# Fewer out-state weights in the attention, power 0 by ScalarE, pointer scalars in norm and softmax, h1 scaled by ScalarE

## The chip, the cores and the metric

The kernel runs on one core of a Trainium2 chip. The metric is device microseconds of one execution. TensorE (PE) multiplies, VectorE (DVE), ScalarE (ACT) and GpSimd (POOL) do the elementwise work, SyncE (SP) issues most of the DMAs. Every engine works through its own instructions in order.

## The reference, cut to what matters

Two layers share a residual stream of 512 latent tokens and 256 context tokens of width 1024, all in float32. Layer 0 is windowed attention with a sink logit (16 heads, 128 wide), layer 1 a bidirectional S5 state space (128 groups of 16 channels, 64 complex states, two directions). Each layer ends in `layer_norm(alpha * x + gate * ((y * silu(z)) @ w_out))`. The softmax takes the sink into its sum:

```python
def softmax_with_sink(s, sink):
    sk = jnp.broadcast_to(sink[None, :, :, None, None], s.shape[:-1] + (1,))
    return jax.nn.softmax(jnp.concatenate([s, sk], -1), axis=-1)[..., :-1]
```

The S5 recurrence is `h[t] = abar * h[t-1] + bbar @ u[t]`, `y[t] = Re(cmat @ h[t])`, from the left and from the right.

## The kernel before, in words

Every float32 product is three matmuls of a high and a low part (`mm3`, lines 155 to 157); the parts are made by a copy on ScalarE and a subtraction on VectorE (lines 145 and 146, 580 and 581). The S5 layer is computed in chunks of 8 tokens. For that it needs *in-state weights* (`gen_w`, 64 of them) and *out-state weights* (`gen_o`, 32 of them, indices q = 0 to 31), which depend on parameters alone and are built while layer 0 runs, mostly on GpSimd, and stored to device memory.

An out-state weight q takes two loads on SyncE's queue, gcb (line 905) and gpp, the powers 0 to 8 of the states (line 907); three small products for gbb (lines 919 to 921); and for each of two directions d three instructions over 4 x 9 x 16 = 576 elements (lines 931 to 933) that multiply coefficients with the nine powers into a tile gO, with a scratch tile gX that has one buffer. In the powers' table power 0 stands at place 0 for d = 0 and at place 8 for d = 1; its first part is +1 on partitions 0 to 63 and -1 on 64 to 127, its second part is 0. Eight of the nine places, all but power 0, go to device memory (line 936). A later step, `lag` (lines 941 to 958), multiplies gbb with eight of the nine places of gO on TensorE (line 948), adds on VectorE and stores a tile gK (line 958); after every eighth weight, eight more DMAs move the collected gK (line 974). Weights 3, 7 and 11 run on VectorE, the others on GpSimd.

Layer 0 has 48 attention pieces (8 pairs of heads, 6 blocks of queries), between which the projections are interleaved. Pieces 1 to 21 carry in-state weights. From piece 22 (`NW`) on, `bg` opens a pool "go" (`open_o`, with four buffers of gO) and issues out-state weights up to `min(QA, (n - NW + 1) * QA // (47 - NW))` after piece n; each new weight is followed by the lag of the one before it. In `att_s` a piece computes scores, their negative maximum nm (for the context blocks by lines 453 and 454), the exponentials and their sums (line 461), adds the sink's exponential (lines 463 and 464), takes the reciprocal and scales.

The output projection follows (`outproj0`): half 0 of the columns for blocks 0, 1, 2 together, then 3, 4 and 5; half 1 for 5, 4, 0 together, then 1, 2 and 3. After each block's body it calls `side`, which in its first `NB` calls issues the remaining out-state weights, from a second pool "go2" with three buffers of gO; the pool is closed with the last. When both halves of a block are there, `norm` takes mean and variance, and the reciprocal root by three Newton steps on one column per partition (lines 293 and 294); line 631 normalizes, and `make_h1` transposes the block, applies scale and shift (four of eight pieces on VectorE, line 1018, four on ScalarE, line 1020) and splits it (lines 1023 and 1024) for the input projection of layer 1 (`uproj_ctx`, `uproj`). The tiles U of that projection come from a pool "uu" that is opened on the same side of memory after go2 is closed.

The whole program is put in order by a scheduler with a cost model: a priority is the place in the program, and `high_priority` with a negative offset (-80 for weights, -50 for lags) moves an instruction back. It fixes each engine's order before the run; tiles that share memory bring waits with them.

Of the kernel before, what the change touches and what calls it, by code (L numbers as in the profile page):

```python
# [111 lines left out]
F32 = mybir.dt.float32  # L112
# [21 lines left out]
class K:  # L134
# [141 lines left out]
    def norm(self, rs, pool):  # L276
        nc = self.nc
        st = pool.tile([128, 3, 6], F32, name="st")
        for i, (r, _) in enumerate(rs):
            nc.vector.bn_stats(st[:, i], r)  # L280
        mv = pool.tile([128, 2], F32, name="mv")
        nc.vector.bn_aggr(mv, st[:, :len(rs)])

        xe = pool.tile([128, 3], F32, name="xe")
        nc.vector.scalar_tensor_tensor(xe, mv[:, 1:2].to_broadcast([128, 3]), 1e-5, self.nscale, op0=ALU.add, op1=ALU.mult)
        ih = pool.tile([128, 2], I32, name="ih")
        nc.vector.tensor_scalar(ih[:, 0:1], xe[:, 2:3].bitcast(I32), 1, None, op0=ALU.logical_shift_right)
        nc.vector.tensor_scalar(ih[:, 1:2], ih[:, 0:1], -1, MAGIC_Y, op0=ALU.mult, op1=ALU.add)
        y = ih[:, 1:2].bitcast(F32)
        nt = pool.tile([128, 6], F32, name="nt")  # L290
        for i in range(3):
            t, yn = nt[:, 2 * i:2 * i + 1], nt[:, 2 * i + 1:2 * i + 2]
            nc.vector.scalar_tensor_tensor(t, y, xe[:, i:i + 1], y, op0=ALU.mult, op1=ALU.mult)
            nc.vector.scalar_tensor_tensor(yn, t, -3.0, y, op0=ALU.add, op1=ALU.mult)
            y = yn
        return mv[:, 0:1], y

# [33 lines left out]
def layer0(k, bg, early, late):  # L331
# [92 lines left out]
    def att_s(p, q, kk, qb):  # L424

        lat = qb < 4
        kb0, kb1 = (max(0, qb - 1), min(4, qb + 2)) if lat else (0, 0)
        win = list(range(kb0, kb1))

        cols = win + [4, 5]  # L430
        nw = 128 * len(win)
        n = nw + 256
        qs = slice(qb * 128, qb * 128 + 128)
        mc = k.sp.tile([128, 2], F32, name="mx", bufs=8)
        nm = k.sp.tile([128, 2], F32, name="nm", bufs=8)
        sm = k.sp.tile([128, 2], F32, name="sm", bufs=8)
        P = [k.sp.tile([128, 640], F32, name="P", bufs=2 * DEPTH + 2) for h in range(2)]

        def scores(h, S, cs, m, o):
            mm3(S, q[h][0][:, qs], q[h][1][:, qs], kk[0][:, cs], kk[1][:, cs], True, True)  # L440
            w = cs.stop - cs.start
            if lat:

                first = o == nw
                nc.vector.tensor_tensor_reduce(P[h][:, o:o + w], S, mask[:, m:m + w], -SCALE,  # L445
                                               k.nsink[:, 2 * p + h:2 * p + h + 1] if first else mc[:, h:h + 1],
                                               op0=ALU.add, op1=ALU.min, accum_out=(mc if first else nm)[:, h:h + 1])
        Sc = k.ps.tile([128, 2, 256], F32, name="S", tag="S", bufs=2)
        for h in range(2):
            scores(h, Sc[:, h], C, 384, nw)  # L450
        hs = slice(2 * p, 2 * p + 2)
        if not lat:
            nc.vector.tensor_reduce(mc, Sc, axis=AX.X, op=ALU.max)
            nc.vector.scalar_tensor_tensor(nm, mc, -SCALE, k.nsink[:, hs], op0=ALU.mult, op1=ALU.min)
        for h in range(2 if lat else 0):
            Sw = k.ps.tile([128, 512], F32, name="S", tag="S", bufs=2)[:, :nw]
            scores(h, Sw, slice(kb0 * 128, kb1 * 128), 128 if qb == 0 else 0, 0)
        es = k.sp.tile([128, 2], F32, name="es", bufs=8)
        for h in range(2):
            src = P[h][:, :n] if lat else Sc[:, h]  # L460
            nc.scalar.activation(P[h][:, :n], src, AF.Exp, bias=nm[:, h:h + 1], scale=-1.0 if lat else SCALE, accum_out=sm[:, h:h + 1])  # L461
        for h in range(2):
            nc.scalar.activation(es[:, h:h + 1], nm[:, h:h + 1], AF.Exp, bias=k.sink[:, 2 * p + h:2 * p + h + 1])
        nc.vector.tensor_add(es, es, sm)
        nc.vector.reciprocal(es, es)  # L465
        for h in range(2):
            nc.scalar.activation(P[h][:, :n], P[h][:, :n], AF.Copy, scale=es[:, h:h + 1])  # L467
        return P, cols
# [423 lines left out]
def open_o(k, pool, q0, q1, gob):  # L892

    k.gob, k.dq = gob, q0
    k.dd = pool.tile([128, 16 * (q1 - q0)], F32, name="dd")
    k.nc.sync.dma_start(k.dd, k.a["dd"][:, 16 * q0:16 * q1])


def gen_o(k, pool, q):

    nc, a = k.nc, k.a
    n = DO if q < DQ else DP
    eng = nc.vector if q % n == n - 1 else nc.gpsimd
    cb = pool.tile([128, 4, 2, 4, 16], F32, name="gcb", bufs=2)
    nc.sync.dma_start(cb.rearrange("p t d g n -> p (t d g n)"), a["cb"][q])
    pp = pool.tile([128, 2, 80], F32, name="gpp", bufs=2)
    nc.sync.dma_start(pp, k.ppsc[q])
    dd = k.dd
    O = []
    bb = pool.tile([128, 8, 2, 16], F32, name="gbb", bufs=2)  # L910
    t = pool.tile([128, 4, 9, 16], F32, name="gX", bufs=1).rearrange("p g k n -> p (g k n)")
    by, bx = (t[:, 128 * i:128 * i + 128].rearrange("p (d g n) -> p d g n", d=2, g=4) for i in range(2))

    def qb(o):
        return pp[:, :, o:o + 4][:, :, :, None].to_broadcast([128, 2, 4, 16])

    def dup(t):
        return t.rearrange("p d g n -> p (d g) n")[:, :, None].to_broadcast([128, 8, 2, 16])
    eng.tensor_tensor(by, cb[:, 2], qb(72), op=ALU.mult)
    eng.tensor_tensor(bx, cb[:, 3], qb(76), op=ALU.mult)  # L920
    eng.tensor_tensor(bb, dup(by), dup(bx), op=ALU.add)
    for d in range(2):
        o = pool.tile([128, 4, 9, 16], F32, name="gO", bufs=k.gob)
        x = pool.tile([128, 4, 9, 16], F32, name="gX", bufs=1)

        def cc(t):
            return cb[:, t, d][:, :, None].to_broadcast([128, 4, 9, 16])

        def pb(o_):
            return pp[:, d, o_:o_ + 36].rearrange("p (g k) -> p g k", g=4)[:, :, :, None].to_broadcast([128, 4, 9, 16])  # L930
        eng.tensor_tensor(o, cc(0), pb(0), op=ALU.mult)  # L931
        eng.tensor_tensor(x, cc(1), pb(36), op=ALU.mult)  # L932
        last = eng.tensor_tensor(o, o, x, op=ALU.add)  # L933
        O.append(o)
        x0 = 1 - d
        nc.sync.dma_start(k.osc[q, :, :, :, d].rearrange("p u r x -> p (u r) x"),
                          o[:, :, x0:x0 + 8].rearrange("p g t n -> p g (t n)"))

    def lag(after=None):
        ps = k.ps.tile([128, 512], F32, name="lag", tag=k.lagtag[0], bufs=k.lagtag[1])  # L940

        def lh(d, g):
            return bb[:, 4 * d + g].rearrange("p a n -> p (a n)")

        for d in (1, 0):
            for g in range(4):
                rs = slice(32 * g, 32 * g + 32)
                m = nc.tensor.matmul(ps[rs, 128 * (1 - d):128 * (1 - d) + 128], lh(d, g), O[d][:, g, d:d + 8], start=True, stop=True)  # L948
                if g == 0 and d == 1 and after is not None and k.gob > 3:

                    k.tc.add_manual_dep(ins_of(m), ins_of(after).name,
                                        mybir.DependencyInfo(mybir.DependencyClass.NoSync, mybir.DependencyReason.DATA), reason="lag")
        K_ = pool.tile([128, 240], F32, name="gK", bufs=1)
        nc.scalar.activation(K_[:, 0:112], ps[:, 0:112], AF.Copy)
        nc.scalar.activation(K_[:, 128:240], ps[:, 144:256], AF.Copy)
        nc.vector.tensor_add(K_[:, 112:128], ps[:, 112:128], dd[:, 16 * (q - k.dq):16 * (q - k.dq) + 16])
        nc.vector.tensor_add(K_[:, 112:128], ps[:, 128:144], K_[:, 112:128])
        nc.sync.dma_start(k.ksc[q], K_)
        if q % 8 == 7:
            gen_m0(k, q // 8)  # L960
    return lag, last
# [42 lines left out]
def make_h1(k, b, n):  # L1004
# [4 lines left out]
    for j in range(2):  # L1009
# [4 lines left out]
        for i in range(4):  # L1014
            kk = 4 * j + i
            g, c = k.h1g[:, r, kk:kk + 1], k.h1b[:, r, kk:kk + 1]
            if j == 0:
                nc.vector.tensor_scalar(hf[:, kk], t[:, i], g, c, op0=ALU.mult, op1=ALU.add)
            else:
                nc.scalar.activation(hf[:, kk], t[:, i], AF.Identity, bias=c, scale=g)  # L1020
    H, Lo = k.H1[r]
    ts = slice((b - 4 * r) * 128, (b - 4 * r) * 128 + 128)
    nc.scalar.activation(H[:, :, ts], hf, AF.Copy)
# [308 lines left out]

N0, NW, EW = 1, 22, 8
QO, QN = 32, 1
QA, NB = 27, 3
PP = 300
GP = 80
XP = 100
# [251 lines left out]
```

## Time and profile before

| | |
|---|---|
| median of 3 runs | 1510.47 us (1504.64 to 1512.83) |
| the profiled execution's own time | 1508.56 us |
| its span | 1506.8 us |
| TensorE busy | 1404.2 us, 93% |
| VectorE busy | 1040.2 us, 69% |
| ScalarE busy | 645.8 us, 43% |
| GpSimd busy | 635.0 us, 42% |
| mean granted TensorE clock | 0.971 |

The span is from the first to the last instruction of the profiled execution. In the rows, PE, DVE, ACT, POOL and SPq are TensorE, VectorE, ScalarE, GpSimd and SyncE's queue; L933 is line 933 of the kernel; `gO<-gcb,gpp` means that gO is written and gcb and gpp are read. "Idle before, <- releaser" is the time that an engine stood still before an instruction, and what ended it. The clock is a share of full speed. The attention runs to about 670 us, the output projection to about 870 us, and layer 1 takes the rest; from 870 us on GpSimd has next to nothing to do until the last projection.

### The profile page before, as it was taken

Reading aid. Unit: us, or ns where it says so; the run is one execution under the profiler, and the core shown is the slowest. Engines: PE = TensorE matmul, PEld = TensorE weight load, DVE = VectorE, ACT = ScalarE, POOL = GpSimd, SP = SyncE. Lnnn points to the kernel's source line nnn. Section 1 sums busy time; section 2 is a strip of 40 time slices with the busy share of each in tenths; the row PEclk is TensorE's granted clock in tenths of the full one; section 3 lists DMA queues with packets and bytes.
Section 4 is the critical chain, followed back from the end, with each engine's and each line's share of the span. In section 5 each row is a group of like instructions: output and inputs, shape, how many; then the busy total and the mean of one; then the engine's idle time right before and its main releaser. Section 6 shows DMA issues by size and latency. Waiting matters only on the chain.

```text
span 1506.8 us, 25662 instructions
## 1 busy us (share of the span) xinstructions
PE 1404.2 (93%) x9092; PEld 1134.5 (75%) x9092; DVE 1040.2 (69%) x2711; ACT 645.8 (43%) x1256; POOL 635.0 (42%) x542
## 2 busy tenths in 40 slices
PE   7999999999997899987988799999999999999997
PEld 2554789988886788875766688888777777888886
DVE  7734748777684477876759922789887896565376
ACT  1310546555464446552333234445556545343220
POOL 0004469999998676988975800000000000000240
PEclk9999999999998899998999899999999999999999
DMA  9876566766664446488795476667666796655541
GB/s 335 274 232 203 163 192 202 225 214 208 200 221 152 131 146 200 141 248 265 214 280 158 137 257 226 210 210 231 220 226 220 223 292 213 197 195 168 180 152 60
DMA packets 252639, 309.57 MB, mean 205 GB/s; under 512 B 45408, under 2 KB 151648, under 8 KB 252512
## 3 DMA queue, kind: packets, MB, share of 16 engines
q1 hardware_dynamic: 227168, 295.36, 61.5%
q10 hardware_dynamic: 25344, 12.59, 2.9%
q8 instruction: 71, 1.16, 0.3%
q14 instruction: 56, 0.46, 0.1%
HBM read 239.20 MB, written 77.07 MB: 210 GB/s over the span
## 4 chain that ended last, share of the span: by engine, by line
PE 54%; POOL 13%; DVE 13%; DMA 10%; issue 5%; ACT 3%; SPq 1%; POOLq 0%; DVEq 0%; ACTq 0%
PE pg L155 4%; PE pg L157 4%; PE pg L156 4%; PE adaps L166 3%; PE po L156 3%; PE po L157 3%; PE po L155 3%; DMA wsc<-gW 3%; PE ins L1084 3%; POOL gm L885 3%; POOL gm L886 2%; PE pul L155 2%; PE pul L156 2%; PE pul L157 2%; POOL gW L888 2%
## 5 line engine op out<-in xcount | busy, mean ns | idle before, releaser
L1318 POOL TENSOR_TENSOR xt<-xt,lng 128x512 f32<-128x512 f32 (+1 forms) x9 | 13.7, 1532 | 584.5 <-DMA xt<-n0sc 584.5
L146 DVE TENSOR_TENSOR wl<-wr,wh 128x1024 fp32r<-128x1024 f32 x104 | 137.8, 1325 | 142.9 <-ACT wh L145 140.3
L145 ACT ACTIVATE wh<-wr 128x1024 fp32r<-128x1024 f32 x104 | 109.9, 1057 | 188.0 <-PE pc L156 52.0
L155 PE MATMUL pg<-ga,wh 128*128 128x512 f32 x256 | 100.3, 392 | 0.8 <-ACT ga L1243 0.8
L157 PE MATMUL pg<-ga,wl 128*128 128x512 f32 x256 | 100.5, 393 | 0.0
L933 POOL TENSOR_TENSOR gO<-gO,gX 128x576 f32<-128x576 f32 x58 | 94.9, 1635 | 4.4
L885 POOL TENSOR_TENSOR gm<-gB,gE 128x512 f32<-128x512 f32 x56 | 78.6, 1403 | 23.6 <-DVE zs L500 19.3
L931 POOL TENSOR_TENSOR gO<-gcb,gpp 128x576 f32<-128x576 f32 x58 | 77.0, 1333 | 25.2 <-PE lag L948 20.6
L932 POOL TENSOR_TENSOR gX<-gcb,gpp 128x576 f32<-128x576 f32 x58 | 82.1, 1415 | 2.8
L886 POOL TENSOR_TENSOR gm<-gB,gE 128x512 f32<-128x512 f32 x56 | 82.6, 1475 | 0.0
L461 ACT ACTIVATE P<-P,nm 128x512 f32<-128x512 f32 (+1 forms) x64 | 49.7, 776 | 76.3 <-DVE nm L445 76.2
L487 DVE TENSOR_TENSOR ptl<-PT,pth 128x512 fp32r<-128x512 f32 (+1 forms) x96 | 60.9, 639 | 22.6 <-ACT pth L486 21.9
L1107 DVE TENSOR_TENSOR x<-m 128x64 f32<-128x64 f32 x376 | 74.7, 217 | 2.4
L146 DVE TENSOR_TENSOR gl<-gr,gh 128x512 fp32r<-128x512 f32 x48 | 50.2, 1047 | 31.2 <-ACT gh L145 31.2
L467 ACT ACTIVATE P<-P,es 128x512 f32<-128x512 f32 (+2 forms) x96 | 60.5, 682 | 19.7 <-DVE es L465 19.6
L155 PE MATMUL pq<-hh,wh 128*128 128x512 f32 x160 | 66.0, 413 | 2.8 <-ACT hh L255 2.8
L486 ACT ACTIVATE pth<-PT 128x512 fp32r<-128x512 f32 (+1 forms) x96 | 52.4, 559 | 34.4 <-PE PT L483 26.0
L483 PE MATMUL PT<-ident,P 128*128 128x128 f32 x352 | 61.3, 282 | 6.2 <-DVE vl L388 2.8
L155 PE MATMUL po<-woh,gh 128*128 128x512 f32 (+1 forms) x156 | 59.9, 394 | 7.5 <-ACT woh L580 4.7
L156 PE MATMUL pq<-hl,wh 128*128 128x512 f32 x160 | 65.8, 412 | 0.8 <-DVE hl L256 0.8
L157 PE MATMUL pq<-hh,wl 128*128 128x512 f32 x160 | 64.9, 406 | 0.3 <-DVE wl L146 0.3
L156 PE MATMUL po<-wol,gh 128*128 128x512 f32 (+1 forms) x156 | 61.7, 395 | 3.5 <-DVE wol L581 3.5
(317 smaller groups left out, 4673.2 us busy)
## 6 DMA issues: line engine op xcount, KB each, us to landing
wr<-w SPq DMA_DIRECT2D x40, 512.0 KB
osc<-gO SPq DMA_DIRECT2D x64, 256.0 KB
wr<-wout SPq DMA_DIRECT2D x32, 512.0 KB
W<-wsc SPq DMA_DIRECT2D x32, 512.0 KB
om<-osc SPq DMA_DIRECT2D x64, 256.0 KB
wr<-glu SPq DMA_DIRECT2D x32, 512.0 KB
gE<-esc SPq DMA_DIRECT2D x56, 256.0 KB
gB<-bt SPq DMA_DIRECT2D x56, 256.0 KB
```

The source lines that it names most:

```text
L145: nc.scalar.activation(hi, raw, AF.Copy)
L146: nc.vector.tensor_sub(lo, raw, f32(hi))
L155: mm(out, wh, mh, start=start, stop=False)
L156: mm(out, wh, ml, start=False, stop=False)
L157: mm(out, wl, mh, start=False, stop=stop)
L483: nc.tensor.transpose(T[:, j, h, :], P[h][:, c * 128:(c + 1) * 128], k.ident)
L885: tt(x(m1), x(B), eb(0), op=ALU.mult)
L886: tt(x(m2), x(B), eb(1), op=ALU.mult)
L931: eng.tensor_tensor(o, cc(0), pb(0), op=ALU.mult)
L932: eng.tensor_tensor(x, cc(1), pb(36), op=ALU.mult)
L933: last = eng.tensor_tensor(o, o, x, op=ALU.add)
L1107: nc.vector.tensor_add(x, m[:, :, 0], m[:, :, 1])
```

## The change

The Newton steps of `norm`, the minimum with the sink and the sum of the softmax become `tensor_scalar` instructions whose second operand is a pointer scalar (one value per partition); the two-column ones become two of one column. In `gen_o` the three large instructions cover only the eight places that are not power 0; that place is written by a copy on ScalarE with a sign per partition, for which `open_o` loads a small tile sg. In `make_h1` all eight pieces are scaled on ScalarE. `QA`, the number of out-state weights in the attention, goes from 27 to 20, and `NB`, the number of calls of `side` over which the rest is spread, from 3 to 5.

```diff
--- before.py
+++ after.py
@@ -290,8 +290,8 @@
         nt = pool.tile([128, 6], F32, name="nt")
         for i in range(3):
             t, yn = nt[:, 2 * i:2 * i + 1], nt[:, 2 * i + 1:2 * i + 2]
-            nc.vector.scalar_tensor_tensor(t, y, xe[:, i:i + 1], y, op0=ALU.mult, op1=ALU.mult)
-            nc.vector.scalar_tensor_tensor(yn, t, -3.0, y, op0=ALU.add, op1=ALU.mult)
+            nc.vector.tensor_scalar(t, y, xe[:, i:i + 1], y, op0=ALU.mult, op1=ALU.mult)
+            nc.vector.tensor_scalar(yn, t, -3.0, y, op0=ALU.add, op1=ALU.mult)
             y = yn
         return mv[:, 0:1], y
 
@@ -448,10 +448,11 @@
         Sc = k.ps.tile([128, 2, 256], F32, name="S", tag="S", bufs=2)
         for h in range(2):
             scores(h, Sc[:, h], C, 384, nw)
-        hs = slice(2 * p, 2 * p + 2)
         if not lat:
             nc.vector.tensor_reduce(mc, Sc, axis=AX.X, op=ALU.max)
-            nc.vector.scalar_tensor_tensor(nm, mc, -SCALE, k.nsink[:, hs], op0=ALU.mult, op1=ALU.min)
+            for h in range(2):
+                nc.vector.tensor_scalar(nm[:, h:h + 1], mc[:, h:h + 1], -SCALE, k.nsink[:, 2 * p + h:2 * p + h + 1],
+                                        op0=ALU.mult, op1=ALU.min)
         for h in range(2 if lat else 0):
             Sw = k.ps.tile([128, 512], F32, name="S", tag="S", bufs=2)[:, :nw]
             scores(h, Sw, slice(kb0 * 128, kb1 * 128), 128 if qb == 0 else 0, 0)
@@ -461,7 +462,8 @@
             nc.scalar.activation(P[h][:, :n], src, AF.Exp, bias=nm[:, h:h + 1], scale=-1.0 if lat else SCALE, accum_out=sm[:, h:h + 1])
         for h in range(2):
             nc.scalar.activation(es[:, h:h + 1], nm[:, h:h + 1], AF.Exp, bias=k.sink[:, 2 * p + h:2 * p + h + 1])
-        nc.vector.tensor_add(es, es, sm)
+        for h in range(2):
+            nc.vector.tensor_scalar(es[:, h:h + 1], es[:, h:h + 1], sm[:, h:h + 1], None, op0=ALU.add)
         nc.vector.reciprocal(es, es)
         for h in range(2):
             nc.scalar.activation(P[h][:, :n], P[h][:, :n], AF.Copy, scale=es[:, h:h + 1])
@@ -894,6 +896,9 @@
     k.gob, k.dq = gob, q0
     k.dd = pool.tile([128, 16 * (q1 - q0)], F32, name="dd")
     k.nc.sync.dma_start(k.dd, k.a["dd"][:, 16 * q0:16 * q1])
+    sg = pool.tile([128, 2], F32, name="sg")
+    k.nc.sync.dma_start(sg, k.a["sgn"])
+    k.sg = sg[:, 0:1]
 
 
 def gen_o(k, pool, q):
@@ -924,13 +929,16 @@
         x = pool.tile([128, 4, 9, 16], F32, name="gX", bufs=1)
 
         def cc(t):
-            return cb[:, t, d][:, :, None].to_broadcast([128, 4, 9, 16])
+            return cb[:, t, d][:, :, None].to_broadcast([128, 4, 8, 16])
 
         def pb(o_):
-            return pp[:, d, o_:o_ + 36].rearrange("p (g k) -> p g k", g=4)[:, :, :, None].to_broadcast([128, 4, 9, 16])
-        eng.tensor_tensor(o, cc(0), pb(0), op=ALU.mult)
-        eng.tensor_tensor(x, cc(1), pb(36), op=ALU.mult)
-        last = eng.tensor_tensor(o, o, x, op=ALU.add)
+            return pp[:, d, o_:o_ + 36].rearrange("p (g k) -> p g k", g=4)[:, :, 1 - d:9 - d][:, :, :, None].to_broadcast([128, 4, 8, 16])
+
+        nc.scalar.activation(o[:, :, 8 * d], cb[:, 0, d], AF.Copy, scale=k.sg)
+        o8, x8 = o[:, :, 1 - d:9 - d], x[:, :, 0:8]
+        eng.tensor_tensor(o8, cc(0), pb(0), op=ALU.mult)
+        eng.tensor_tensor(x8, cc(1), pb(36), op=ALU.mult)
+        last = eng.tensor_tensor(o8, o8, x8, op=ALU.add)
         O.append(o)
         x0 = 1 - d
         nc.sync.dma_start(k.osc[q, :, :, :, d].rearrange("p u r x -> p (u r) x"),
@@ -1014,10 +1022,7 @@
         for i in range(4):
             kk = 4 * j + i
             g, c = k.h1g[:, r, kk:kk + 1], k.h1b[:, r, kk:kk + 1]
-            if j == 0:
-                nc.vector.tensor_scalar(hf[:, kk], t[:, i], g, c, op0=ALU.mult, op1=ALU.add)
-            else:
-                nc.scalar.activation(hf[:, kk], t[:, i], AF.Identity, bias=c, scale=g)
+            nc.scalar.activation(hf[:, kk], t[:, i], AF.Identity, bias=c, scale=g)
     H, Lo = k.H1[r]
     ts = slice((b - 4 * r) * 128, (b - 4 * r) * 128 + 128)
     nc.scalar.activation(H[:, :, ts], hf, AF.Copy)
@@ -1332,7 +1337,7 @@
 
 N0, NW, EW = 1, 22, 8
 QO, QN = 32, 1
-QA, NB = 27, 3
+QA, NB = 20, 5
 PP = 300
 GP = 80
 XP = 100
```

## Rows read from the trace of the kernel before

**Rows 1.** The page's first part: busy time, share of the span, instructions.
```profile
PE 1404.2 (93%) x9092; PEld 1134.5 (75%) x9092; DVE 1040.2 (69%) x2711; ACT 645.8 (43%) x1256; POOL 635.0 (42%) x542
```

**Rows 2.** Windows: stretch, length, engines' busy time, PE clock, DMA share, GB/s.
```profile
470.00:510.00 40.00, 24.71 (x169) 21.37 (x168) 17.06 (x49) 15.10 (x36) 27.96 (x27) 0.81 0.50 156
510.00:650.00 140.00, 138.11 (x1045) 121.31 (x1044) 104.88 (x229) 82.82 (x220) 108.91 (x97) 0.99 0.52 158
650.00:700.00 50.00, 36.76 (x215) 27.99 (x214) 35.39 (x44) 17.77 (x38) 46.10 (x37) 0.90 0.89 271
...
800.00:870.00 70.00, 53.05 (x357) 45.34 (x359) 68.62 (x138) 22.09 (x47) 55.99 (x45) 0.88 0.45 144
```

**Rows 3.** Timeline of TensorE, 480 to 515 us: start, length, work, [idle before].
```profile
486.87 1.08 PE L948 MATMUL lag<-gO,gbb 128*32 128x128 f32 x16 [8.74 <-POOL gO L933]
...
506.04 0.58 PE L155 MATMUL S<-kh,qh 128*128 128x256 f32 x1 [5.77 <-DVE nm L445]
```

**Rows 4.** Timeline of VectorE, 480 to 515 us.
```profile
503.42 0.29 DVE L919 TENSOR_TENSOR gX<-gcb,gpp 128x128 f32<-128x128 f32 x1 [6.26 <-POOL gO L933]
```

**Rows 5.** Timeline of GpSimd, 474 to 868 us.
```profile
474.41 0.40 POOL L919 TENSOR_TENSOR gX<-gcb,gpp 128x128 f32<-128x128 f32 x1 [5.42 <-DMA gpp<-ppsc]
...
669.78 0.40 POOL L919 TENSOR_TENSOR gX<-gcb,gpp 128x128 f32<-128x128 f32 x1
...
779.89 1.75 POOL L933 TENSOR_TENSOR gO<-gO,gX 128x576 f32<-128x576 f32 x1
805.58 0.87 POOL L919 TENSOR_TENSOR gX<-gcb,gpp 128x128 f32<-128x128 f32 x1 [23.93 <-DVE nt L294]
...
865.37 2.46 POOL L933 TENSOR_TENSOR gO<-gO,gX 128x576 f32<-128x576 f32 x1
```

**Rows 6.** The chain of waits, 600 to 700 us: start, length, what.
```profile
670.56 0.36 SPq L936
...
675.06 6.28 DMA wr<-wout
```

**Rows 7.** Groups of VectorE, 800 to 870 us: busy, mean ns, idle before.
```profile
L631 DVE TENSOR_SCALAR nrm<-R,mv,nt 128x512 f32<-128x512 f32 (+1 forms) x13 | 13.1, 1031 | 0.1
...
L1018 DVE TENSOR_SCALAR h1f<-h1t,h1g,h1b 128x128 f32<-128x128 f32 x24 | 8.2, 396 | 0.0
...
L287 DVE TENSOR_SCALAR ih<-xe 128x1 int32<-128x1 int32 x6 | 0.8, 138 | 0.0
```

**Rows 8.** Windows, 800 to 870 us, of L293 alone, then of L294 alone.
```profile
800.00:870.00 70.00, 9.67 (x18) 0.88 0.45 144
...
800.00:870.00 70.00, 7.34 (x18) 0.88 0.45 144
```

**Rows 9.** Groups of VectorE, 1410 to 1507 us.
```profile
L293 DVE SCALAR_TENSOR_TENSOR nt<-nt,xe 128x1 f32<-128x1 f32 x8 | 1.7, 218 | 0.2
```

**Rows 10.** Groups of GpSimd, whole span, shapes apart.
```profile
L933 POOL TENSOR_TENSOR gO<-gO,gX 128x576 f32<-128x576 f32 x58 | 94.9, 1635 | 4.4
...
L932 POOL TENSOR_TENSOR gX<-gcb,gpp 128x576 f32<-128x576 f32 x58 | 82.1, 1415 | 2.8
L885 POOL TENSOR_TENSOR gm<-gB,gE 128x512 f32<-128x512 f32 x56 | 78.6, 1403 | 23.6 <-DVE zs L500 19.3
L931 POOL TENSOR_TENSOR gO<-gcb,gpp 128x576 f32<-128x576 f32 x58 | 77.0, 1333 | 25.2 <-PE lag L948 20.6 <-PE h1t L1013 4.4
```

**Rows 11.** Groups of ScalarE, whole span, shapes apart.
```profile
L1020 ACT ACTIVATE h1f<-h1t,h1b,h1g 128x128 f32<-128x128 f32 x24 | 9.1, 457 | 32.9 <-PE h1t L1013 25.5 <-DVE H1L L1024 4.7 <-PE po L157 2.7
...
L954 ACT ACTIVATE gK<-lag 128x112 f32<-128x112 f32 x32 | 8.3, 259 | 24.3 <-PE lag L948 18.0 <-DVE gl L146 2.5 <-DMA m0sc<-ksc 1.6
```

**Rows 12.** Groups of VectorE, whole span, shapes apart.
```profile
L464 DVE TENSOR_TENSOR es<-es,sm 128x2 f32<-128x2 f32 x48 | 22.6, 470 | 13.4 <-ACT es L463 13.0 <-ACT P L461 0.2
...
L454 DVE SCALAR_TENSOR_TENSOR nm<-mx,nsink 128x2 f32<-128x2 f32 x16 | 9.0, 562 | 0.2
```

**Rows 13.** Timeline of SyncE's queue, 440 to 560 us.
```profile
469.38 0.42 SPq L896 DMA_DIRECT2D dd<-dd  x1
```

## Prediction

> **What bounds the kernel now.** I read the busy shares first: TensorE has work in 93% of the span [rows 1], so time is lost only where it stands still or runs at a lower clock. Then the windows by stage [rows 2]. Between 510 and 650 us, the middle of the attention, TensorE is busy 138.11 of 140 us: whatever VectorE, ScalarE or GpSimd save there is covered. Three stretches near it are different. At 470 to 510 us it has 24.71 of 40 at a granted clock of 0.81; at 650 to 700 us it has 36.76 of 50 at 0.90 while the DMA engines are at 0.89; at 800 to 870 us it has 53.05 of 70 at 0.88, while VectorE has 68.62 of 70. The change touches all three.
>
> The waits of TensorE explain the first one [rows 3]: 8.74 us for the power products of out-state weight 0, whose lag matmuls stand in its queue, and 5.77 us for VectorE, 14.5 us together. VectorE itself stood 6.26 us [rows 4], because weight 3, which it builds, shares the one-buffer scratch tile gX with the weights before it on GpSimd. GpSimd starts weight 0 only at 474.41 us, when the in-state weights are done [rows 5]; so its being late stops two other engines.
>
> For the second, the chain of waits shows SyncE's queue: a write of gO (L936) that waits for GpSimd stands ahead of the store of gK, and the load of the next output weight goes out at 675.06 us behind both [rows 6].
>
> In the third VectorE is the bound, and its rows show with what [rows 7, 8]. The 36 one-column instructions of the norm's iteration (L293, L294) take 9.67 + 7.34 = 17.0 us, 0.47 each. Beside an idle GpSimd the same L293 takes 0.218 [rows 9], and L287, a one-column tensor_scalar in the same crowded window, 0.138. So what costs is two SBUF tensors read beside GpSimd's work, not the arithmetic. L1018, which reads PSUM and two pointer scalars, holds 0.396 in that window.
>
> **The change part by part.** The sum goes against the profiled execution: 1508.56 us (span 1506.8 and 1.8 around it), 1.9 below the median of 1510.47.
>
> *Norm and h1.* In 800 to 870 us the 36 instructions become tensor_scalar with pointer scalars. No row shows one with an SBUF column and a pointer in SBUF. From below, L287's 0.138; from above, 0.47 as now, if the pointer's read stops beside GpSimd too, as the SBUF-to-SBUF L631 of 512 columns does (1.03) [rows 7]. I take L293's undisturbed 0.22, the nearest row in operands: 36 × 0.22 = 7.9, a saving of 9.1 us. The 24 pieces of h1 that leave VectorE are 8.2 us more: 17.3 of its 68.62. ScalarE takes them at 0.457 each at most [rows 11], 11 us on top of 22.09 of 70, so it does not become the bound. But on each of the 6 blocks the two halves of h1 ran side by side, and now eight pieces follow each other on ScalarE: up to 4 × 0.457 = 1.8 us more in a block's own chain, of which VectorE's queue hid most. What is late next is TensorE, with 17 us idle to give, and the chain of the last block. I take two thirds of 17, **11 us**. Bounds: 17 gained, or 4 lost (the columns stay at 0.47, and each of the last two blocks' chains is 1.8 longer).
>
> The Trainium skill advises against the h1 step: "ScalarE: Activation LUTs", section "Rules for kernel authors", would have multiplies and adds on VectorE. By the rule moving them loses (0.457 − 0.396) × 24 = 1.5 us; but the window has VectorE full and ScalarE at 22.09 of 70, so I go by the window.
>
> *Power 0 on ScalarE.* GpSimd's three instructions per direction go from 576 to 512 elements. The best from rows is one ninth of 1333 + 1415 + 1635 ns, twice per weight: 0.97 us. The worst is L885, 512 elements of another access pattern at 1403 ns: then the first two products (1333, 1415) gain nothing, 0.1 lost [rows 10]. I take 0.8, since only the count changes. For 29 weights on GpSimd that is 23 us, none of it on the path by itself. The 64 copies on ScalarE lie between 0.259 (L954, no pointer) and 0.457 (L1020, two pointers) [rows 11]: I take 0.36, 23 us in all, hidden beside 82.82 of 140 busy us in the attention. If that cover went, by ScalarE waiting for a free gO as GpSimd does now, it would cost the 20.6 us that L931 waits for lag matmuls [rows 10]; queued behind such a copy are the exponentials and the splits of transposed probabilities, and TensorE waits for those.
>
> *20 and 12 weights.* Up to 669.78 us 18 weights are done, 15 on GpSimd and weights 3, 7 and 11 on VectorE [rows 5]. With 20 in the attention two are left there, not nine. That acts at both ends. At the start each weight comes later in the program: weight 0 at piece 23 for 22, weight 3 at piece 26 for 25, a piece being about 7.5 us ((665 − 470)/26). If the engines' orders follow this, both stalls nearly go, 14.5 us; if they follow when the scheduler thinks GpSimd is ready, they stay, and the new copy makes ScalarE wait for the same late input. I take **5**. At the seam SyncE's queue has fewer writes to wait for; TensorE's idle time is 13.2, but the DMA engines are at 0.89, so I take **3** of 0 to 8.
>
> In the projection the pace is 12.4 us per weight: 9 from 669.78 to 781.64, 5 from 805.58 to 867.83 [rows 5]. At 11.6 the 12 take 139 us. The second pool opens when the first is done; that took 24 us from last to first instruction (781.64 to 805.58). Weights 18 and 19 end near 685, so the 12 run from about 705 to 844, before the 867.8 of now: cost 0, with no product beside the last norms.
>
> *Softmax.* 48 additions of two columns at 0.470 and 16 minima at 0.562 become pairs [rows 12]: at 0.22 each 0.44 per pair, at 0.138 a pair 0.28, contended 0.94. That is from 11 us less VectorE to 29 more, in a stretch where TensorE has 138.11 of 140. I count 0.
>
> *Small additions.* Two loads of sg on SyncE cost about 0.42 issue each, as the load of dd beside them does [rows 13], ahead of the first weight's inputs: 0.5. In the last norm a pointer more on six dependent instructions: 0.5. Together **+1**.
>
> Sum: −11 − 5 − 3 + 1 = −18. 1508.56 − 18 = 1490.6, so **1490 us**; its own range 1480 to 1500.
>
> **The rivals.**
>
> *A, deeper.* All three stretches give what they have: 17 + 14.5 + 8 = 39.5, so 1469. For it: no stall named here has another cause in the rows. Against it: at 0.89 the DMA engines hold the second, and GpSimd's late start is unchanged.
>
> *B, relief without effect.* Pointer columns stay at 0.47, or the path in 800 to 870 us goes over to transposes and ScalarE, and only 8.2 us of VectorE is gained, half of it on the path: about 4, so 1504. For it: L631 shows a tensor_scalar that is slow beside GpSimd. Against: L1018 and L287 are not. The Trainium skill ("SBUF — State Buffer", section "Who interferes with whom") lists tensor_scalar among the operations that can take the port pair shared with GpSimd, with operands that allow it; L287's 0.138 is against that for one column, and no row here shows it with a pointer.
>
> *C, ScalarE coupled to GpSimd (slower).* Each weight's copy needs gcb and a free gO, both of which came late in the attention, and ScalarE works in order. If the 20.6 us that GpSimd waits now become ScalarE's, and the 8 of the first two stretches go, only 11 of gain stays: 1508.56 + 20.6 − 11 + 1 = 1519. It decides when the waits pass 10 us. Against: GpSimd is less late with 20 weights.
>
> *D, twelve are too many (slower).* If the second pool fills only from about 745 us, after the first group of three blocks, 745 + 139 = 884, 16 later than 867.8, and the in-projection's tiles lie in that pool's memory. With the 11 hidden behind it and 8 gained before: 1508.56 + 16 − 8 + 1 = 1518. It decides from a start past 728 us (867.8 − 139). Against: the 24 us from release to start put it at 705.
>
> **How the numbers follow.** Forecast 0.53, A 0.13, B 0.18, C 0.09, D 0.07. A difference under 0.5%, 7.5 us, can't be told from none here: 1503 to 1518 counts as the same. Faster: the forecast, A and a quarter of B, 0.70. Slower: C and half of D, 0.13. Same: the rest, 0.17. The range goes to A below and stops short of C and D: 1468 to 1512.
>
> **What would show it.** Right: L293 and L294 near 0.2 us at the end of the projection, and VectorE there clearly under full; GpSimd's products at 512 elements near nine tenths of now; the two waits at 470 to 510 us shrunk; the last weight done by about 845 us. Wrong: ScalarE copies of gO (L936 of the new file or near) idle for lag matmuls or gcb; the last weight past 860 us with matmuls behind it; one-column tensor_scalar at 0.4 or more beside GpSimd; VectorE no longer full and yet the in-projection starting at 870 as now.

## The result and the profile after

The changed kernel takes 1486.21 us (median of 4 runs, 1483.56 to 1487.78) against 1508.46 for the kernel before beside it: a ratio of 0.9857, 95% interval 0.9831 to 0.9883. Measured again beside the kernel before, it was 1488.96 us, ratio 0.9866 (0.9843 to 0.9889). Medians are over all runs of a kernel; the ratios leave disturbed runs out. The forecast of 1490 us and its range held the time. Its terms are another matter.

The first view is the windows of the kernel after, by stage, with the columns of [rows 2].

```profile
470.00:510.00 40.00, 33.64 (x212) 29.43 (x213) 27.60 (x74) 26.35 (x68) 27.86 (x29) 0.84 0.50 152
650.00:700.00 50.00, 41.45 (x234) 32.63 (x233) 31.71 (x43) 18.66 (x37) 21.65 (x20) 0.90 0.86 265
800.00:850.00 50.00, 41.61 (x321) 35.38 (x319) 48.26 (x105) 31.16 (x77) 35.76 (x30) 1.00 0.59 179
850.00:870.00 20.00, 18.84 (x132) 18.26 (x131) 3.67 (x3) 7.56 (x15) 0.00 (x0) 1.00 0.81 244
```

VectorE is still full to 850 us. Then it is nearly empty (3.67 of 20 us), GpSimd has nothing left, and TensorE is already in the next stage at a granted clock of 1.00, where 800 to 870 us stood at 0.88 before [rows 2].

The starts of a few matmuls cut the span into stretches: po is the output projection, pul the first product that needs the last block's h1. Each value is from a profiled execution, the second column of after from the second measurement.

| us | before | after | after, again |
|---|---|---|---|
| to the first po | 669.0 | 666.8 | 669.0 |
| first to last po (projection) | 178.4 | 176.3 | 178.4 |
| last po to first pul (turn) | 23.1 | 8.3 | 8.4 |
| first pul to the end | 636.2 | 633.2 | 634.2 |
| span | 1506.8 | 1484.6 | 1489.8 |

So the gain is at the turn, 14.8 us; the rest is 2 to 3 us here and there. The two executions of one and the same program differ by 4.8 us before 471 us already (GpSimd's in-state weights end at 465.65 in one and 470.42 in the other), so 4 us read from two profiles alone prove nothing.

TensorE's timeline of the kernel after, at the start of the out-state weights and at the turn, answers [rows 3]; ScalarE's and GpSimd's follow, for [rows 5].

```profile
473.76 0.58 PE L155 MATMUL O<-pth,vh 128*128 128x256 f32 x1 [12.00 <-ACT zs L499]
...
851.40 0.44 PE L155 MATMUL pul<-H1H,wh 128*128 128x384 f32 x1 [1.16 <-ACT h1f L1025]
```

```profile
469.92 0.59 ACT L937 ACTIVATE gO<-gcb,sg 128x64 f32<-128x64 f32 x2 [15.22 <-DMA gcb<-cb]
```

```profile
671.06 1.37 POOL L924 TENSOR_TENSOR gX<-gcb,gpp 128x128 f32<-128x128 f32 x1 [9.84 <-DMA gpp<-ppsc]
...
704.62 0.40 POOL L924 TENSOR_TENSOR gX<-gcb,gpp 128x128 f32<-128x128 f32 x1 [22.43 <-DMA gpp<-ppsc]
...
836.66 1.27 POOL L941 TENSOR_TENSOR gO<-gO,gX 128x512 f32<-128x512 f32 x1
```

At the start, the stops of 8.74 and 5.77 us became one of 12.00: ScalarE, in order, stands 15.22 us at the first power-0 copy, whose input comes when GpSimd is through with the in-state weights. GpSimd's second batch starts at 704.62 us and ends at 837.9, 30 us earlier than before.

Groups of VectorE (800 to 870 us), GpSimd and ScalarE (460 to 860 us), for [rows 7, 8, 10, 11]:

```profile
L633 DVE TENSOR_SCALAR nrm<-R,mv,nt 128x512 f32<-128x512 f32 (+1 forms) x13 | 10.8, 875 | 0.1
...
L293 DVE TENSOR_SCALAR nt<-nt,xe 128x1 f32<-128x1 f32 x11 | 2.9, 267 | 0.2
...
L294 DVE TENSOR_SCALAR nt<-nt 128x1 f32<-128x1 f32 x11 | 2.2, 204 | 0.2
```

```profile
L941 POOL TENSOR_TENSOR gO<-gO,gX 128x512 f32<-128x512 f32 x58 | 85.2, 1469 | 3.9
L940 POOL TENSOR_TENSOR gX<-gcb,gpp 128x512 f32<-128x512 f32 x58 | 76.5, 1320 | 3.2
L939 POOL TENSOR_TENSOR gO<-gcb,gpp 128x512 f32<-128x512 f32 x58 | 71.5, 1242 | 11.4 <-issue 4.1 <-ACT zt L401 3.6 <-ACT pth L488 1.4
```

```profile
L937 ACT ACTIVATE gO<-gcb,sg 128x64 f32<-128x64 f32 x64 | 21.8, 347 | 30.1 <-DMA gcb<-cb 17.0 <-PE lag L956 4.6 <-issue 4.2
...
L1025 ACT ACTIVATE h1f<-h1t,h1b,h1g 128x128 f32<-128x128 f32 x48 | 17.7, 468 | 5.9 <-DVE H1L L1029 5.8
```

### The profile page after: what moved, and what is told of

It reads as the page before. It is cut to its first block, busy times and chain, and to the rows that moved or that the text cites. A ratio compares the mean times of both kernels' runs of the same rounds, so it can differ in the third digit from the quotient of the medians.

```text
span 1484.6 us, 25841 instructions
## 1 busy us (share of the span) xinstructions
PE 1389.9 (94%) x9092; PEld 1123.2 (76%) x9092; DVE 1016.6 (68%) x2751; ACT 667.6 (45%) x1344; POOL 604.8 (41%) x542
## 5 line engine op out<-in xcount | busy, mean ns | idle before, releaser
L146 DVE TENSOR_TENSOR wl<-wr,wh 128x1024 fp32r<-128x1024 f32 x104 | 142.9, 1374 | 137.7 <-ACT wh L145 135.6
L941 POOL TENSOR_TENSOR gO<-gO,gX 128x512 f32<-128x512 f32 x58 | 85.2, 1469 | 3.9
L940 POOL TENSOR_TENSOR gX<-gcb,gpp 128x512 f32<-128x512 f32 x58 | 76.5, 1320 | 3.2
L146 DVE TENSOR_TENSOR gl<-gr,gh 128x512 fp32r<-128x512 f32 x48 | 53.3, 1113 | 33.8 <-ACT gh L145 33.7
L939 POOL TENSOR_TENSOR gO<-gcb,gpp 128x512 f32<-128x512 f32 x58 | 71.5, 1242 | 11.4 <-issue 4.1
L155 PE MATMUL O<-pth,vh 128*128 128x256 f32 x176 | 53.4, 303 | 20.4 <-ACT zs L499 12.0
L145 ACT ACTIVATE gh<-gr 128x512 fp32r<-128x512 f32 x48 | 30.2, 630 | 71.5 <-DMA gr<-gsc 44.4
```

What stands on the lines that cost most here:

```text
L145: nc.scalar.activation(hi, raw, AF.Copy)
L146: nc.vector.tensor_sub(lo, raw, f32(hi))
L155: mm(out, wh, mh, start=start, stop=False)
L939: eng.tensor_tensor(o8, cc(0), pb(0), op=ALU.mult)
L940: eng.tensor_tensor(x8, cc(1), pb(36), op=ALU.mult)
L941: last = eng.tensor_tensor(o8, o8, x8, op=ALU.add)
```

## The experiments

Two theories. The first is the prediction's: VectorE is relieved at the turn. The second: the last block goes when GpSimd has the last weight ready. Every ratio is to the kernel before, timed beside it.

**Taking one part back.** Four kernels, each the changed kernel less one part.

```diff
# u_norm: the Newton steps as before (the second instruction of a step likewise)
-            nc.vector.tensor_scalar(t, y, xe[:, i:i + 1], y, op0=ALU.mult, op1=ALU.mult)
+            nc.vector.scalar_tensor_tensor(t, y, xe[:, i:i + 1], y, op0=ALU.mult, op1=ALU.mult)
# u_h1: pieces of j == 0 on VectorE again
# u_split
-QA, NB = 20, 5
+QA, NB = 27, 3
# u_pow0: no copy, products of 576 elements
```

> The changed kernel with the norm's Newton steps back as two-tensor instructions (all else changed). Theory 'VectorE relief': the 36 one-column instructions of the projection's last 70 us go back from 0.23 us to about 0.4 to 0.5, so 6 to 9 us of VectorE return where it is full; 1491 to 1495 us, and the time from the last product of the output projection to the first latent product of the in-projection grows from 8 by 3 to 7 us. Rival 'GpSimd done early': with GpSimd finished at 838 us the last two norms run beside an idle GpSimd either way, and only the first four norms cost more, beside products of TensorE: 1486 to 1489 us.

Measured: 1491.97 us, 0.9894 (0.9864 to 0.9925). The time is the first theory's, but the turn did not grow (8.6 us): the loss is in the projection, 184.8 us long.

> The changed kernel with four of eight h1 pieces back on VectorE. Theory 'VectorE relief': 8.2 us of VectorE return in the full stretch, half of it on the path: about 1490 us. Rival 'GpSimd done early': in the last block's chain eight pieces in a row on ScalarE (3.0 us) become two fours side by side (1.5 us), so no loss or a gain: 1484 to 1487 us.

Measured: 1493.81 us, 0.9907 (0.9883 to 0.9932): slower than either theory had it. The turn is 12.1 us.

> The changed kernel with 27 out-state weights in the attention and 5 in the projection over 3 calls, as before. Theory 'VectorE relief': norm and h1 carry the gain, and the split only moves the end of GpSimd's work; 1488 to 1493 us. Rival 'GpSimd done early': its last weight ends past 855 us again, beside the last norms and in front of the in-projection, and 10 to 15 us of the 22 go: 1496 to 1501 us.

Measured: 1493.7 us, 0.9902 (0.9878 to 0.9927): between the two ranges. The last weight ended at 848.68 us, not past 855.

Each of these three is worth 0.3 to 0.5% beside the others. The interval of `u_norm` overlaps those of the changed kernel widely, so its 0.3% is not clear of noise by time alone; those of the other two hardly overlap. And the fourth:

> The changed kernel with power 0 back in GpSimd's products (576 elements, no copies on ScalarE, no sg). Both theories: 12 weights in the projection take 12 x 0.8 = 10 us longer, so the last ends at about 848 us, in front of the first latent product at 851: 'VectorE relief' gives 1486 to 1489 us, 'GpSimd done early' 1490 to 1496 us. ScalarE's wait of 15.2 us for gcb near 470 us goes, and in its place TensorE waits for the lag of weight 0 and VectorE for gX, as before: 0 to 5 us either way.

Measured: 1508.47 us, 1.0003 (0.9985 to 1.0022): without the shorter products nothing of the gain is left. Neither theory had that. TensorE's timeline of u_pow0 shows the last block right behind the last weight:

```profile
869.09 1.08 PE L950 MATMUL lag<-gO,gbb 128*32 128x128 f32 x16 [1.88 <-POOL gO L935]
870.10 0.69 PE L155 MATMUL pul<-H1H,wh 128*128 128x384 f32 x1
```

**One part alone, and the changed kernel again.** The parts depend on each other, so each had to be seen without the others.

> The changed kernel itself, measured beside the kernels of this set so that effects of 4 to 7 us can be read against the same chip. Both theories expect 1486 us (1483 to 1490), the last weight's lag products near 838 us and the first product of the last block near 851 us.

Measured: 1488.96 us, 0.9866 (0.9843 to 0.9889), lag at 842.6 and pul at 855.7 us.

> The kernel before with only the split changed to 20 and 12. Theory 1 (the gain comes from VectorE being relieved, the split gives a few us at 470 and at 650 to 700 by itself): 1500 to 1505 us. Theory 2 (the last block goes when GpSimd has the last out-state weight ready; twelve weights with products of 576 elements end later than five did): 1512 to 1522 us, the last weight's lag products at 872 us or later and the first product of the last block right behind them.

Measured: 1521.51 us, 1.0077 (1.0059 to 1.0094), in the second theory's range, with the place that it names. GpSimd's timeline, then TensorE's:

```profile
733.48 0.40 POOL L919 TENSOR_TENSOR gX<-gcb,gpp 128x128 f32<-128x128 f32 x1 [22.78 <-DMA gpp<-ppsc]
...
881.35 2.26 POOL L933 TENSOR_TENSOR gO<-gO,gX 128x576 f32<-128x576 f32 x1
```

```profile
885.66 1.08 PE L948 MATMUL lag<-gO,gbb 128*32 128x128 f32 x16 [0.67 <-DVE gK L957]
886.68 0.69 PE L155 MATMUL pul<-H1H,wh 128*128 128x384 f32 x1
```

This is rival D, in a kernel that has only half of the change: a second batch that starts past 728 us. At 12.5 us a weight it ends 16 us later than in the kernel before.

> The kernel before with only power 0 on ScalarE and products of 512 elements; the split stays 27 and 5. Theory 1 (products off the path): 1504 to 1509 us. Theory 2 (the supply of the last weights sets the end of the attention): the last five weights start with the same transfer near 805 us and end some 4 to 8 us earlier than 870 us, 1499 to 1504 us. If the ScalarE's first copy stands waiting for its coefficients at 470 us as in the changed kernel, a few us of that are lost again in both.

Measured: 1499.78 us, 0.9943 (0.9927 to 0.9959), in the second theory's range. The last lag products stand at 865.8 us, only 4.4 earlier than before, and pul at 868.8 waits 1.60 us for ScalarE's h1, not for the weight.

**The other two corners.** `a_pow0split` has split and power 0, `a_normh1` has norm, softmax and h1 (three edits, called N below).

> The kernel before with the split 20 and 12 and power 0 on ScalarE; norm, softmax and h1 as before. So far, against the kernel before: the split alone +13.0 us, power 0 alone -8.7 us. If the two only add: 1512 to 1514 us. Theory 2 (the last block goes at the later of two things, the last weight's lag products and VectorE's norm and h1 of the last block; the shorter products bring twelve weights in before VectorE is through): the last lag products at 843 to 852 us, the first product of the last block 10 us or more behind the last po, 1494 to 1501 us.

Measured: 1496.92 us, 0.9927 (0.9902 to 0.9953). The last lag products stand at 848.3, pul at 860.8, 12.1 behind the last po: the second theory.

> The kernel before with the norm, softmax and h1 edits alone; split 27 and 5, products of 576 elements. Theory 1 (VectorE's relief is worth what it is worth wherever it stands): 1495 to 1502 us, since the same three edits took 13.0 us off the kernel with the split alone. Theory 2 (in the kernel before the last block goes right behind the last weight's lag products at 870 us, which these edits hardly move): 1503 to 1509 us, the first product of the last block again within 1 us of the last lag products.

Measured: 1515.82 us, 1.0038 (1.0016 to 1.0061): slower than either theory had it. TensorE's timeline says why relief is worth nothing here:

```profile
878.94 1.08 PE L950 MATMUL lag<-gO,gbb 128*32 128x128 f32 x16 [8.30 <-POOL gO L935]
879.95 0.69 PE L155 MATMUL pul<-H1H,wh 128*128 128x384 f32 x1
```

VectorE had the last norm ready at 868.9 us; TensorE then stood 8.30 us for GpSimd's last weight. That this came 11 us later than in the kernel before is GpSimd's stream: its first weight starts at 477.82 for 474.41 us, the first 24 weights take 13.2 us each for 12.8, and the last batch starts at 817.77 for 805.58. Why they take longer stays open.

All eight corners (S: split, P: power 0; S with N is `u_pow0`, P with N is `u_split`), with the stretches of their profiled executions (last lag: the start of the last weight's last lag matmul; the last row is the changed kernel's second measurement):

| parts | ratio | projection | last lag | first pul | turn |
|---|---|---|---|---|---|
| none | 1 | 178.4 | 870.2 | 870.6 | 23.1 |
| N | 1.0038 | 186.1 | 879.6 | 880.0 | 25.5 |
| S | 1.0077 | 191.3 | 886.3 | 886.7 | 23.6 |
| P | 0.9943 | 179.6 | 865.8 | 868.8 | 21.0 |
| S, N | 1.0003 | 189.8 | 869.8 | 870.1 | 14.6 |
| P, N | 0.9902 | 181.8 | 850.9 | 860.1 | 11.9 |
| S, P | 0.9927 | 183.0 | 848.3 | 860.8 | 12.1 |
| S, P, N | 0.9866 | 178.4 | 842.6 | 855.7 | 8.4 |

In the first three and in S with N, pul starts within 0.5 us of the last weight's lag products; in P 3.0 behind. That does not yet say what it waited for. TensorE's timeline of the kernel before, then ScalarE's:

```profile
864.33 1.92 PE L1013 MATMUL h1t<-ident,nrm 128*128 128x128 f32 x6 [4.21 <-DVE nrm L631]
868.03 0.69 PE L1013 MATMUL h1t<-ident,nrm 128*128 128x128 f32 x2 [1.78 <-DVE nrm L631]
869.56 1.08 PE L948 MATMUL lag<-gO,gbb 128*32 128x128 f32 x16 [0.84 <-DVE gK L957]
870.57 0.69 PE L155 MATMUL pul<-H1H,wh 128*128 128x384 f32 x1
```

```profile
868.76 1.51 ACT L1020 ACTIVATE h1f<-h1t,h1b,h1g 128x128 f32<-128x128 f32 x4 [8.16 <-PE h1t L1013]
```

TensorE waits for VectorE's last norm, and the 0.84 us before the lag products end with an addition on VectorE. ScalarE's pieces of h1, which end the wait before pul in P and in S, P, end here at 870.27 us, 0.3 before pul (in S at 886.54, 0.1 before). So in the kernel before and in S the last weight itself held pul for 0.3 us at most: the second theory is not borne out there as it was put. TensorE stands for GpSimd's gO only in N (8.30 us) and in S with N (1.88). In P and in the last three it waits 1.16 to 2.25 us for ScalarE's h1.

Why the turn halves when GpSimd is early, with VectorE's instructions unchanged, shows in VectorE's groups, first of the kernel before (847 to 871 us), then of `a_pow0split` (848 to 861 us):

```profile
L631 DVE TENSOR_SCALAR nrm<-R,mv,nt 128x512 f32<-128x512 f32 (+1 forms) x5 | 7.0, 1417 | 0.1
...
L294 DVE SCALAR_TENSOR_TENSOR nt<-nt 128x1 f32<-128x1 f32 x4 | 2.5, 624 | 0.1
L293 DVE SCALAR_TENSOR_TENSOR nt<-nt,xe 128x1 f32<-128x1 f32 x3 | 2.5, 822 | 0.1
```

```profile
L631 DVE TENSOR_SCALAR nrm<-R,mv,nt 128x512 f32<-128x512 f32 (+1 forms) x5 | 2.2, 488 | 0.0
...
L293 DVE SCALAR_TENSOR_TENSOR nt<-nt,xe 128x1 f32<-128x1 f32 x3 | 0.7, 217 | 0.1
L294 DVE SCALAR_TENSOR_TENSOR nt<-nt 128x1 f32<-128x1 f32 x3 | 0.5, 153 | 0.1
```

The same code, but for one step of L294, takes 12.0 us in the one and 3.4 in the other: GpSimd is at work through the first to 867.8 us and done at 846.4 us in the second. So GpSimd holds the last block of the kernel before by slowing VectorE, not by its last weight.

**The stop at 470 us.** Three kernels went at the 12.00 us that ScalarE's early copy costs TensorE.

```diff
# p0early: the first two weights' copies on GpSimd
-        nc.scalar.activation(o[:, :, 8 * d], cb[:, 0, d], AF.Copy, scale=k.sg)
+        if q < 2:
+            nc.gpsimd.tensor_scalar(o[:, :, 8 * d], cb[:, 0, d], k.sg, None, op0=ALU.mult)
+        else:
+            nc.scalar.activation(o[:, :, 8 * d], cb[:, 0, d], AF.Copy, scale=k.sg)
# p0late: for q < 2 the copies stand in lag(), ordered behind the next weight's last product
# held: for q < 2 the copies, and weight 0's lag products, ordered behind a later
# unit's scaled P; the weights are written into the program from piece 30 on
-                    out_q(min(QA, (n - NW + 1) * QA // (47 - NW)), n == 47)
+                    out_q(min(QA, max(0, n - 30) * QA // (47 - 30)), n == 47)
```

> The changed kernel, with the power-0 copies of the first two out-state weights made by GpSimd instead of ScalarE. If ScalarE's 15.2 us wait for the first coefficients at 470 us is what stops TensorE for 12.0 us there, that wait goes, TensorE is stopped for 2 to 9 us (by GpSimd's first weight, as before), and the kernel takes 1479 to 1484 us. If the stop is set by the transfers alone, it stays at 10 to 13 us and the time at 1486 us.

Measured: 1497.15 us, 0.9921 (0.9903 to 0.9939). The stop became 8.3 us for GpSimd's gO and 2.9 for VectorE. TensorE's and ScalarE's orders moved in many places, so why it is 8 us worse than the changed kernel stays open.

> The changed kernel, with the power-0 copies of the first two out-state weights put behind the products of the weight that follows each, so that ScalarE doesn't stand waiting for the first coefficients at 455 to 475 us. If that wait is what stops TensorE for 10 to 12 us there, ScalarE's wait goes, TensorE's longest stop at 470 to 510 us falls to 6 us or less, and the kernel takes 1479 to 1484 us. If GpSimd's start of the out-state weights is the limit, another stop of about 10 us takes its place and the time stays at 1486 to 1490 us.

Measured: 1492.99 us, 0.9895 (0.9867 to 0.9923), 3 us above the second expectation's range. ScalarE's first copy waits only 3.87 us, and another stop of TensorE takes the place, as that expectation had it:

```profile
489.26 1.08 PE L962 MATMUL lag<-gO,gbb 128*32 128x128 f32 x16 [11.13 <-POOL gO L941]
```

The edit had a price of its own: held longer, the coefficients' buffers came free late, and ScalarE stood 15.68 us for the third weight's at 497.73 us.

> The changed kernel, with the power-0 copies of the first two out-state weights and the lag products of the first placed some ten units of attention later in the engines' orders (on TensorE 62 rows later), so that neither ScalarE nor TensorE reaches them before GpSimd's first weights are there. The products of GpSimd are not moved in its own order. If standing in order ahead of GpSimd's late start is what costs the 10 to 12 us at 470 to 490 us, TensorE's longest stop there falls to 4 us or less, the last po comes 5 to 10 us earlier, the last weight's lag products (838 to 843 us) are then what the last block waits for, and the kernel takes 1479 to 1485 us. If the stop only moves (the next weights' products are waited for instead), 1486 to 1492 us.

Measured: 1507.03 us, 0.9972 (0.9953 to 0.9991). TensorE's longest stop at 470 to 510 us is 2.70 us, it has 37.30 busy us of 40 there, and the last po comes at 836.8, 10.5 us before that of the changed kernel in its second measurement. So far it is as the first expectation had it. But the last lag products come at 868 us, not 838 to 843, and the time is 18 us above the changed kernel's and far outside both ranges, since the last weight slipped. GpSimd's timeline, then TensorE's:

```profile
736.91 0.40 POOL L929 TENSOR_TENSOR gX<-gcb,gpp 128x128 f32<-128x128 f32 x1 [27.30 <-DMA gpp<-ppsc]
...
866.13 1.26 POOL L948 TENSOR_TENSOR gO<-gO,gX 128x512 f32<-128x512 f32 x1
```

```profile
867.44 1.08 PE L963 MATMUL lag<-gO,gbb 128*32 128x128 f32 x16 [6.41 <-POOL gO L948]
868.46 0.69 PE L155 MATMUL pul<-H1H,wh 128*128 128x384 f32 x1
```

TensorE was 10 us ahead through the attention and gave it all back at the turn, which is 31.7 us long. The edit also moved GpSimd's stream: its first 17 weights take 13.8 us each for 12.4 in the changed kernel's second measurement, and up to 720 us its products into gO wait 18.3 us for ScalarE instead of 6.2. What the stop costs with that stream unmoved, no run shows. No version beat the changed kernel.

## Why the prediction was right, and where it was not

**The time** was right, 1486 to 1489 for 1490. That the sum came out is in part luck: of its −18 the −5 of the start and the −3 of the seam are not to be seen in the profiles, and what power 0 gave, entered at 0, stood in for them. Two of its terms came by another road than the text gave.

**Norm and h1, −11 us:** right in size, but only with the other parts. From S, P to S, P, N the ratio falls from 0.9927 to 0.9866 or 0.9857, some 9 to 11 us (softmax, counted 0, is in it); from S to S, N they gain 11 too, from P to P, N 6, and alone the same edits cost 6. In S they also bring GpSimd's second batch from 12.5 to 11.9 us a weight, so part of the relief comes back through GpSimd. The text had them as relief of VectorE in 800 to 870 us "and the chain of the last block", whatever GpSimd did. The split of the term is visible where one edit is undone. With the norm as before, the projection takes 184.8 us (183.0 in S, P) for 176.3 and 178.4, and the turn stays 8.6: in these profiles, one of each kernel, the norm's edit pays where GpSimd works beside it, from 705 to 838 us. With half of h1 on VectorE the projection stays 176.6 and the turn is 12.1: h1 is worth 3.8 us at the turn. Once GpSimd is done, the pointer form is even slower than the old one, 0.272 and 0.214 us for 0.217 and 0.153.

**Power 0, "none of it on the path by itself":** this step failed. Saved were 91, 95 and 166 ns per instruction, 0.70 us per weight, where 0.8 was taken, and the copies took 0.347 for 0.36. But the turn depends on when GpSimd's stream of weights ends, and that is its length up to the second batch, the wait for that batch's memory, and then 12 weights. Without the shorter products (S, N) the second batch starts at 725.88 instead of 704.62 and 707.54 us and its 12 weights take 11.9 us each instead of 11.1 and 11.2, and the last one ends at 869 instead of 838 and 842. The 0.70 us a weight make 20 of these 27 to 31 us over the 29 on GpSimd; where the rest comes from was not traced. The first pul comes 14 to 19 us earlier, and the ratios 1.0003 and 0.9866 lie 20 apart. The prediction had computed the end of the last weight (844; it was 837.9) and the point from which it decides (728) for rival D alone, and counted its coming 24 us early, "with no product beside the last norms", as 0. It is worth the 11 us between the turns of none and S, P (23.1 and 12.1), above all because VectorE's last chain runs without GpSimd: 3.4 us for 12.0.

**The start, −5:** not shown. The two stops became one of 12.00 us, by rival C's mechanism at one place (ScalarE in order behind gcb); the first po came 0 to 2.2 us earlier. The run `held` shows that the 12 are worth nothing when GpSimd's last weight slips for them; what they are worth without that slip is open.

**The seam, −3:** from the last pzl to the first po it was 12.0 us before, 15.5 and 13.1 after. No gain.

**The signs named beforehand.** L293 and L294 near 0.2: yes. Products near nine tenths: 0.90 to 0.93. The last weight by 845 us: yes. VectorE clearly under full: no, 48.26 of 50 us to 850; it ends earlier, it isn't idler. Waits at 470 us shrunk: 14.5 to 12.0. One sign of being wrong came true: ScalarE's copies of gO stood 17.0 us for gcb and 4.6 for lag matmuls.

**A slip in the working.** At 0.28 us a pair the softmax takes 18 us for the 31.6 of before, 14 less and not 11; the term was counted 0 either way.

**Rivals.** C's condition, a wait past 10 us, was met by the 15.22 us at 470 us, but its price did not follow: TensorE's stop there did not grow. B's pointer column stayed fast beside GpSimd, 0.267 and 0.204. The Trainium skill, "SBUF — State Buffer", section "Who interferes with whom", says that a VectorE instruction with two SBUF inputs contends with a GpSimd one that reads SBUF, and that a tensor_scalar, with operands that allow its two-port mode, contends with GpSimd, the one that issues first holding the shared ports for its whole instruction; the trace agrees in that both are slower beside GpSimd: the two-input column (0.822 us, 0.217 without) and the 512-column tensor_scalar (1.417 and 0.488). The Trainium skill, "ScalarE: Activation LUTs", section "Rules for kernel authors", would have the multiply and add of the h1 step on VectorE; here it cost 0.468 us a piece on ScalarE for 0.396 and yet gained, where VectorE was the fuller engine.

## What to carry to other kernels

When a side engine feeds the end of a stage, follow its stream to the last item first: any saving per item is multiplied by all items before that one, while time won on the main engine upstream is given back if that stream slips. Then see by the waits how its end holds the stage: here less by the last item itself than by the engine that it slowed until then. Edits on one path of several don't add: test the corners, since undoing one of them may show the whole gain and doing it alone may show a loss. And where one engine slows its neighbour, that ends when it ends, so finishing it early can be worth more than lightening the neighbour.

## What the runs showed of the hardware

The size of the exclusion was not expected: beside GpSimd's products of 1.3 to 1.6 us on average, a one-column instruction with two SBUF tensors took up to 1.37 us (L293 of the kernel before, at 816.82 us) for 0.217 without, six times as long; with a pointer in place of the second tensor the same step took 0.204 to 0.272 on average in both cases. And GpSimd's in-state weights ended 4.8 us apart in two executions of one program; the first po came 2.1 us apart and the first pul 4.3.
